# A hybrid decoder step on one core: third head's operands and first loads moved, results of empty slots not stored, two tiles of the per-layer embedding beside the routing, the rest of it in a fixed order

## The chip, the cores and the metric

The kernel runs on one core of a Trainium2 chip. A core has five engines with an instruction queue each: TensorE (PE, matrix products; its weight loads are listed as PEld), VectorE (DVE), ScalarE (ACT), GpSimd (POOL) and SyncE (SP, here an issuer of DMAs). They work from on-chip memory (SBUF), products land in PSUM banks, and 16 DMA engines move data between SBUF and DRAM. The metric is the device time of one execution in microseconds; the time of a kernel is the median of its runs.

## What is computed

One step of a one-layer decoder for 1,024 prompt tokens and 64 sample tokens (8 sequences of 8), width 1,024, all in float32:

```python
h = rmsnorm(x); P = h @ w_in
mix = concat(rwkv7(P), dilated_window_attention(P))     # 8 heads of 64 each
x = x + mix @ w_out
# 1 of 4 groups, then 2 of 8 experts in it: 32 experts of width 256
x = x + sum over the 2 experts of w * (silu(h2 @ w_gate) * (h2 @ w_up)) @ w_down
x = x + (p @ w_ple) * sigmoid(rmsnorm(x) @ w_ple_gate)  # per-layer embedding, p of width 256
y = rmsnorm(x)
```

It also returns the recurrent state and the windows of keys and values. Each token goes to two experts, so 2,176 rows are routed.

## The kernel before

Products are done in three passes: each operand is split into a high part (ACT, L54) and a low part (DVE, L55), and `mm3` (L1348) adds high by high, high by low and low by high. The stages, in order of time:

- Projections (to about 430 us), then the RWKV recurrence in chunks for the prompt. `chain` multiplies the state by its decay on POOL (L779, kept as `self.decay`); a tile of 256 tokens ends with its group norm, whose scale is L871 on POOL.
- Attention of the sample tokens, then of the prompt. The prompt's attention runs in two calls of `phase3`: heads 0 and 1 for the first five blocks, then all heads in pairs, interleaved with the recurrence of the sample tokens (`phase2s`). For each head `head` loads k (L992) and two halves of q (L995) by POOL's queue; a load of 128x1x1024 is 512 KB. Two buffers (`qk3`) serve heads 0, 1, 3, 4, 6, 7, and a pool of its own (`qx3`, on the left side of SBUF) heads 2 and 5. The scores are L1095, bias and maximum L1098, exp L1107, transposes L1118. Before pair `AHEAD` = 2 a hook closes the recurrence's pools and starts the loads of the next stage.
- Output projection and router for nine tiles of tokens. `pre` is a list of weight loads placed one a tile. The last `route` turns logits into experts, weights and ranks (rank products L1499, the weights' exp L1523) and gives `idx`, the token of each expert's slot. Then a branch on the largest count (`overflow`), for experts with more than `CAP` = 96 tokens.
- The experts, a loop written out in order by `phase5`. For each expert POOL gathers 96 rows of the normed tokens (L1611; rows of empty slots are dropped by the bounds check), PE transposes them (L1624), multiplies by gate and up, transposes, and multiplies by `w_down`; ACT copies the result to one of three buffers (`out`, L1661), and POOL stores 96 rows (L1663) to the array `YE` in DRAM. Weights come by SP's queue three experts ahead (L1305, L1306) and, for `w_down`, four (L1330).
- The tail. `embed` multiplies the nine tiles of p by `w_ple` (12 products a tile, copies by ACT L1601 and DVE L1599, stores to `PL`). For each tile POOL gathers its two result rows a token (L1810), DVE adds them (L1819), and norm (L1824, `hp`), transposes (L1834), split (`hh`, `hl`) and the gate product by `w_ple_gate` (`whg`, `whh` and their low parts) follow. The scheduler of the tile framework places these; only `phase5` fixes its order by hand (`self.ordered`, `o`).

The tile framework adds the waits: an instruction waits for the last readers or writers of the memory that it overwrites, and each DMA takes the next of eight semaphores of its kind (DMASW for POOL's, DMAHW for the others).

## Time and profile before

| | |
|---|---|
| runs | 1543.29, 1542.76, 1533.67 us (median 1542.76) |
| the profiled execution | 1534.7 us, span 1533.0 us |
| PE, DVE, ACT, POOL busy | 90%, 62%, 49%, 25% of the span |
| DMA | 344.63 MB, mean 225 GB/s |
| granted clock of PE, mean | 0.951 of full speed |

Times in the views are microseconds from the start of the span. Engines work in their queue's order; in brackets behind a row stands how long the engine was idle before it and what it waited for. Windows give busy time of each engine with the number of its instructions, then PE's granted clock (1.00 is 2.4 GHz, 0.50 is 1.2 GHz), the DMA engines' mean busy share and the rate.

### The profile page before, as it was taken

Reading aid. Unit: us, or ns where it says so; the run is one execution under the profiler, and the core shown is the slowest. Engines: PE = TensorE matmul, PEld = TensorE weight load, DVE = VectorE, ACT = ScalarE, POOL = GpSimd, SP = SyncE. Lnnn points to the kernel's source line nnn. Section 1 sums busy time; section 2 is a strip of 40 time slices with the busy share of each in tenths; the row PEclk is TensorE's granted clock in tenths of the full one; section 3 lists DMA queues with packets and bytes.
Section 4 is the critical chain, followed back from the end, with each engine's and each line's share of the span. In section 5 each row is a group of like instructions: output and inputs, shape, how many; then the busy total and the mean of one; then the engine's idle time right before and its main releaser. Section 6 shows DMA issues by size and latency. Waiting matters only on the chain. (4 is left out here: it accounts for less than half of the span.)

```text
span 1533.0 us, 24768 instructions
## 1 busy us (share of the span) xinstructions
PE 1373.5 (90%) x9127; PEld 1129.0 (74%) x9128; DVE 957.5 (62%) x2146; ACT 749.3 (49%) x1368; POOL 375.6 (25%) x391
## 2 busy tenths in 40 slices
...
DMA  6145566999578465339888755555999999997551
GB/s 212 42 159 170 170 194 196 318 313 311 160 190 221 132 183 162 115 88 158 137 185 248 260 167 177 198 200 197 382 391 384 388 388 390 372 367 241 188 171 69
DMA packets 254271, 344.63 MB, mean 225 GB/s; under 512 B 103918, under 2 KB 183088, under 8 KB 253617
## 3 DMA queue, kind: packets, MB, share of 16 engines
...
q14 instruction: 53, 0.43, 0.1%
...
## 5 line engine op out<-in xcount | busy, mean ns | idle before, releaser
L270 PE MATMUL pj<-hT_hi,wh 128*128 128x384 f32 (+1 forms) x600 | 199.2, 334 | 4.7 <-DVE lora L278 2.7
L270 PE MATMUL pj<-hT_hi,wl 128*128 128x384 f32 (+1 forms) x600 | 199.0, 332 | 0.0
L270 PE MATMUL pj<-hT_lo,wh 128*128 128x384 f32 (+1 forms) x600 | 198.4, 331 | 0.0
L270 PEld LDWEIGHTS pj<-hT_hi,wh 128*128 128x128 f32 x600 | 113.8, 190 | 6.6 <-DVE lora L278 3.0
L270 PEld LDWEIGHTS pj<-hT_hi,wl 128*128 128x128 f32 x600 | 114.0, 190 | 2.4 <-issue 2.2
L270 PEld LDWEIGHTS pj<-hT_lo,wh 128*128 128x128 f32 x600 | 114.2, 190 | 0.6 <-issue 0.2
L690 DVE TENSOR_TENSOR ftmp<-At,X 128x60 f32<-128x60 f32 (+24 forms) x248 | 57.2, 243 | 54.7 <-DMA At<-ABd 18.2
L1611 POOL DMA_INDIRECT x<-HN,idx x32 | 38.3, 1198 | 204.8 <-PE p4t L1624 195.5
L55 DVE TENSOR_TENSOR dl<-draw,dh 128x1024 fp32r<-128x1024 f32 x66 | 80.0, 1216 | 3.6 <-ACT dh L54 3.6
L1095 PE MATMUL pS<-k,q 128*128 128x512 f32 (+2 forms) x192 | 53.7, 393 | 21.7 <-DMA q<-QP 21.1
L54 ACT ACTIVATE dh<-draw 128x1024 fp32r<-128x1024 f32 x66 | 69.0, 1050 | 8.0 <-DMA draw<-in_w_down_dram 8.0
L55 DVE TENSOR_TENSOR wl<-w,wh 128x1024 fp32r<-128x1024 f32 x25 | 35.2, 1408 | 45.0 <-ACT wh L54 44.2
L692 DVE TENSOR_TENSOR X<-X,ftmp 128x60 f32<-128x60 f32 (+24 forms) x248 | 60.4, 256 | 4.2
L779 POOL TENSOR_TENSOR s<-S,pc 128x512 f32<-128x512 f32 x16 | 16.9, 1055 | 180.5 <-DVE S L798 74.3
L1098 DVE CUSTOM_DVE_ANT_0 s<-pS,bias 128x512 f32<-128x512 f32 (+2 forms) x96 | 50.2, 554 | 11.6 <-PE pS L1095 7.9
L1122 ACT ACTIVATE pt<-pxt 128x512 f32<-128x512 f32 (+3 forms) x64 | 32.4, 514 | 50.7 <-PE pxt L1118 50.5
L1118 PE MATMUL pxt<-ident,s 128*128 128x128 f32 x288 | 48.2, 291 | 9.4 <-DVE pt L1120 5.9
L1107 ACT ACTIVATE s<-s,nm 128x128 f32<-128x128 f32 (+7 forms) x64 | 49.2, 770 | 13.3 <-DVE nm L1103 6.8
L1095 PEld LDWEIGHTS pS<-k,q 128*128 128x128 f32 x192 | 32.4, 204 | 30.7 <-issue 22.7
L1348 PE MATMUL p4y<-dh,hh 128*96 128x512 f32 x128 | 54.0, 422 | 0.7 <-ACT hh L54 0.7
L1348 PE MATMUL p4y<-dh,hl 128*96 128x512 f32 x128 | 50.5, 395 | 0.0
L1348 PE MATMUL p4y<-dl,hh 128*96 128x512 f32 x128 | 50.3, 393 | 0.0
...
## 6 DMA issues: line engine op xcount, KB each, us to landing
...
```

The source lines that it names most:

```text
L54: self.hi = self.o(e.activation(hi, src, AF.Copy) if e is nc.scalar else e.tensor_copy(hi, src))
L55: return self.o((lo_eng or nc.vector).tensor_tensor(lo, src, hi.bitcast(F32), op=ALU.subtract))
L270: nc.tensor.matmul(p[:, :nn], a[:, k, :], b[:, k, n0:n0 + nn], start=(m == 0), stop=(m == 23))
L690: nc.vector.tensor_tensor(o, At[:, t, t + 1:32][:, :, None].to_broadcast([128, m, c]), X[:, t, None, 0:c].to_broadcast([128, m, c]), op=AL ...
L692: nc.vector.tensor_tensor(X[:, t + 1:32, 0:c], X[:, t + 1:32, 0:c], o, op=ALU.add)
L1095: nc.tensor.matmul(ps[:, :n], q[:, a, i * 128:(i + 1) * 128], k[:, c0:c0 + n], start=(a == 0), stop=(a == 1))
L1098: nc.vector.tensor_tensor_reduce(s[:, c0:c0 + n], ps[:, :n], bias[:, bo:bo + n], 1.0, -3e38, ALU.add, ALU.max, m)
L1107: ex = nc.scalar.activation(s[:, :nb * 128], s[:, :nb * 128], AF.Exp, bias=nm, accum_out=den)
L1118: nc.tensor.transpose(px[:, b, :], s[:, (b0 + b) * 128:(b0 + b + 1) * 128], self.ident)
L1122: nc.scalar.activation(pt[:, b0:b0 + m, :], px[:, :m, :], AF.Copy)
L1348: self.o(self.nc.tensor.matmul(p, a[x][:, k, :], w, start=(k == 0 and q == 0), stop=(k == kn - 1 and q == 2)))
L1611: d = nc.gpsimd.indirect_dma_start(out=X[e][:n], out_offset=None, in_=self.HN, in_offset=bass.IndirectOffsetOnAxis(ap=self.idx[:, e:e + 1] ...
```

## The change

1. The six arrays of the recurrence in DRAM become views of one tile `R6`, and `YE` becomes its first part.
2. The store of an expert's result becomes a scatter by `row`: row number for a filled slot, a number past the end for an empty one, which the bounds check drops. `row` comes from two more DVE operations behind the routing.
3. `qx3` moves to the right side, and a new pool `qy3` serves head 5, which is loaded only at the hook. The first loads of heads 0 and 1 are ordered ahead of the last decay, and their second parts behind the last tile's scale (L871).
4. `w_ple` is loaded ahead of the routing, and with it tiles 0 and 1 of the embedding are done there; the loads of `w_down` move by one expert, and `w_ple` is loaded again behind the last expert.
5. `embed` does tiles 2 to 8 in a fixed order, with the splits of the first half of `w_ple_gate` between them; its first transposes go into the last step of the experts.

```diff
-        self.XV = t("XV", [4, 128, T])
+        self.R6 = t("R6", [6, 4, 128, T])
+        self.XV = self.R6[0]
         self.ARd = t("ARd", [4, 128, 17, 128])
-        self.KB = t("KB", [4, 128, T])
-        self.BB = t("BB", [4, 128, T])
+        self.KB = self.R6[1]
+        self.BB = self.R6[2]
         self.PC = t("PC", [4, 128, 24])
-        self.BV = t("BV", [4, 128, T])
-        self.AA = t("AA", [4, 128, T])
-        self.GG = t("GG", [4, 128, T])
+        self.BV = self.R6[3]
+        self.AA = self.R6[4]
+        self.GG = self.R6[5]
...
-        nc.gpsimd.tensor_tensor(yv, yv, r[:n, :, None].to_broadcast([n, 8, 64]), op=ALU.mult)
+        m = nc.gpsimd.tensor_tensor(yv, yv, r[:n, :, None].to_broadcast([n, 8, 64]), op=ALU.mult)
+        if t0 == NP - 256:
+            self.scaled = m
...
-            self.qx = ea.enter_context(self.pool("qx3", side="left"))
+            self.qx = e2.enter_context(self.pool("qx3", side="right"))
...
         def after(d):
-            if a:
-                self.tc.add_manual_dep(d.ins, self.decay.ins.name, mybir.DependencyInfo(mybir.DependencyClass.NoSync, mybir.DependencyReason.DATA))
+            x, y = (d, self.scaled) if a else (self.decay, d)
+            if h < 2:
+                self.tc.add_manual_dep(x.ins, y.ins.name, mybir.DependencyInfo(mybir.DependencyClass.NoSync, mybir.DependencyReason.DATA))
         d = nc.gpsimd.dma_start(k[:, a:w], part(self.KP, [[512 * NP, 2], [NP, 64]]))
...
+                    self.qx = P("qy3")
...
-                        self.head(w[0], w[2])
+                        if w[0] != 5 or p == AHEAD:
+                            self.head(w[0], w[2])
...
+    row[:, 149] = j
...
-        self.YE = d.tile([NE * CAP, D], F32, name="YE")
+        self.YE = self.R6.rearrange("s p q t -> (s p q t)")[0:NE * CAP * D].rearrange("(r c) -> r c", c=D)
...
-        r = self.dr[(j // 2 + 1) % 2 if j > 3 else 0].tile([128, 2, D], F32, tag="r", name="draw")
+        r = self.dr[((j + 1) // 2 + 1) % 2 if j > 2 else 0].tile([128, 2, D], F32, tag="r", name="draw")
         if j <= NE:
-            self.hold(self.o(nc.sync.dma_start(r, (I['w_down'][0, j] if j < NE else I['w_ple'][0]).rearrange("(k p) f -> p k f", p=128))), after)
+            self.hold(self.o(nc.sync.dma_start(r, (I['w_down'][0, j] if 0 <= j < NE else I['w_ple'][0]).rearrange("(k p) f -> p k f", p=128))), after)
...
-        pre = [Dn(0), W(0, 0), W(0, 1), Dn(1), W(1, 0), W(1, 1), Dn(2), Dn(3)]
+        pre = [Dn(-1), W(0, 0), W(0, 1), Dn(0), W(1, 0), W(1, 1), Dn(1), Dn(2)]
...
-                    self.split_d((s - 5) // 2, k)
+                    self.split_d((s - 7) // 2, k)
...
+        pe = p4.tile([128, 2, 256], F32, name="pe4")
+        nc.sync.dma_start(pe, I['p_prompt'][0, 0, 0:256].rearrange("(i p) c -> p i c", p=128))
+        self.emb_trans(0, pe, 128, wk.tile([128, 2, 4, 128], F32R, tag="t1", name="ehl"))
         nc.vector.tensor_scalar(self.idx, pidx[:CAP, 0:NE], float(FREE), None, op0=ALU.add)
+        free = p4.tile([CAP, NE], F32, name="free")
+        nc.vector.tensor_scalar(free, pidx[:CAP, 0:NE], 0.0, float(NE * CAP), op0=ALU.is_ge, op1=ALU.mult)
+        nc.vector.scalar_tensor_tensor(self.row, free, row[:CAP], ist[:CAP], op0=ALU.add, op1=ALU.add)
         pr = self.pst("h")
         nc.tensor.matmul(pr[:, :32], ones, macc, start=True, stop=True)
         nc.vector.tensor_copy(self.cnt, pr[:, :32])
+        for i in range(2):
+            self.emb(i, -1, wk.tile([128, D], F32, tag="t3", name="ple"), False)
...
+    def emb_trans(self, j, pe, n, hl):
+        p = self.pst("t").rearrange("p (a b) -> p a b", b=128)
+        m = 4 if j < 4 else 2
+        for q in range(m):
+            self.o(self.nc.tensor.transpose(p[:, q, :n], pe[:n, q // 2, (q % 2) * 128:(q % 2) * 128 + 128], self.ident[:n, :n]))
+        self.split(hl[:, 0, :m, :n], hl[:, 1, :m, :n], p[:, :m, :n])
+        self.E[j] = hl
+    def emb(self, i, w, o, dve=True):
+        nc = self.nc
+        t0, n = TT[i]
+        a = self.E[i // 2][:, :, 2 * (i % 2):2 * (i % 2) + 2, :n]
+        for j in range(2):
+            c = slice(512 * j, 512 * j + 512)
+            p = self.pst("y")
+            self.mm3(p[:n], (a[:, 0], a[:, 1]), self.Dn[w], 0, 2, 2, c)
+            if j and dve:
+                self.o(nc.vector.tensor_copy(o[:n, c], p[:n]))
+            else:
+                self.o(nc.scalar.activation(o[:n, c], p[:n], AF.Copy))
+        self.o(nc.scalar.dma_start(self.PL[t0:t0 + n, :], o[:n]))
+    def embed_first(self):
+        self.emb_trans(1, self.Dn[NE + 1][:, 2:4], 128, self.w2.tile([128, 2, 4, 128], F32R, tag="t5", name="ehl"))
...
     def embed(self):
-        nc, I, wk = self.nc, self.I, self.wk
+        nc, I = self.nc, self.I
         pes = self.Dn[NE + 1]
-        pe8 = self.r4.tile([128, 256], F32, tag="pe", name="pe8", bufs=1)
-        nc.sync.dma_start(pe8[:NS], I['p_sample'][0].rearrange("b t d -> (b t) d"))
+        pe8 = self.r4.tile([128, 1, 256], F32, tag="pe", name="pe8", bufs=1)
+        nc.sync.dma_start(pe8[:NS, 0], I['p_sample'][0].rearrange("b t d -> (b t) d"))
+        self.load_w(NE)
         O = [self.dh.tile([128, 2, D], F32, tag=t, name="ple") for t in "hl"]
...
+        self.ordered = True
+        for i in range(2, 9):
             if i % 2 == 0 and i < 8:
...
+                j = i // 2 + 1
+                self.emb_trans(j, pes[:, 2 * j:2 * j + 2] if j < 4 else pe8, 128 if j < 4 else NS,
+                               self.w2.tile([128, 2, 4, 128], F32R, tag=("t4", "t5")[j % 2], name="ehl"))
+            self.emb(i, NE, O[i // 2 % 2][:, i % 2])
+            if i < 6:
+                self.split_w(NE, i - 2)
+        self.ordered = False
...
-                self.o(nc.gpsimd.dma_start(self.YE[e * n:e * n + n, :], y[:n]))
+                self.o(nc.gpsimd.indirect_dma_start(out=self.YE, out_offset=bass.IndirectOffsetOnAxis(ap=self.row[:, e:e + 1], axis=0),
+                                                    in_=y[:n], in_offset=None, bounds_check=NE * CAP - 1, oob_is_err=False))
...
+        self.load_d(3)
         self.load_d(4)
-        self.load_d(5)
...
-                if e > 1:
+                if e > 0:
                     self.split_d(e, 0)
                 act(e)
...
+            if last:
+                self.embed_first()
+            if e > 0:
                 self.split_d(e, 1) if not last else [self.split_d(e, k) for k in range(2)]
-            if e > 1 and e + 4 <= NE + 1:
+            if e > 0 and e + 4 <= NE + 1:
                 self.load_d(e + 4)
             if ahead:
...
-            self.load_w(NE)
-            for q in range(4):
-                self.split_w(NE, q)
-                self.hold(self.hi, self.last_hh)
             self.load_w(NE + 1)
```

The built order of POOL, between the recurrence of the prompt and that of the samples. k and q are the operands of a head (7962 and 7956 are the third head's), o and LAK belong to the recurrence, ux to the samples'. Before:

```order
L871 TENSOR_TENSOR y<-y,gnr 128x512
L881 TENSOR_TENSOR o_5985<-o_5985,gb 128x512
L659 TENSOR_TENSOR LAK<-LAK,cst 128x512
L992 DMA k_7962<-KP 128x1x1024
L995 DMA q_7963<-QP 128x1x1024 x2
L992 DMA k_8084<-KP 128x1x1024
L995 DMA q_8085<-QP 128x1x1024 x2
L844 TENSOR_TENSOR ux<-vt_99,cst 64x512 x2
L844 TENSOR_TENSOR ux<-us,cst 64x512 x2
L992 DMA k_8208<-KP 128x1x1024
```

And of the change (its lines are two to five further down; 8779 is the sixth head's k):

```order
L873 TENSOR_TENSOR y<-y,gnr 128x512
L997 DMA k_7956<-KP 128x1x1024
L1000 DMA q_7957<-QP 128x1x1024 x2
L885 TENSOR_TENSOR o_5979<-o_5979,gb 128x512
L997 DMA k_8779<-KP 128x1x1024
L661 TENSOR_TENSOR LAK<-LAK,cst 128x512
L1000 DMA q_8780<-QP 128x1x1024 x2
L997 DMA k_8078<-KP 128x1x1024
L1000 DMA q_8079<-QP 128x1x1024 x2
L846 TENSOR_TENSOR ux<-vt_93,cst 64x512 x2
L846 TENSOR_TENSOR ux<-us,cst 64x512 x2
```

The third head's three loads stand ahead of o and LAK instead of behind them, and the sixth head's come next, ahead of the fourth's (8084 before, 8078 now).

POOL at the end of the experts, with waits, from the last but one gather (x) on. Before, y is stored:

```order
L1611 DMA x_14422<-HN,idx 96x1024 [waits DMASW1_49,PE_49]
L1663 DMA YE<-y_14398 96x1024 [waits DMASW0_49,Activation_49]
L1611 DMA x_14526<-HN,idx 96x1024 [waits DMASW3_49,PE_49]
L1663 DMA YE<-y_14502 96x1024 [waits DMASW2_49,Activation_49]
L1663 DMA YE<-y_14606 96x1024 [waits Activation_49]
L1663 DMA YE<-y_14700 96x1024 [waits DMASW4_49,Activation_49]
L1663 DMA YE<-y_14792 96x1024 [waits DMASW5_49,Activation_49]
L1663 DMA YE<-y_14852 96x1024 [waits DMASW6_49,Activation_49]
L1663 DMA YE<-y_14883 96x1024 [waits DMASW7_49,Activation_49]
```

And of the change, where R is the array `R6`:

```order
L1642 DMA x_14530<-HN,idx 96x1024 [waits DMASW7_49,PE_49]
L1694 DMA R_67<-y_14292,row 3072x1024 [waits DMASW4_49,Activation_49]
L1642 DMA x_14636<-HN,idx 96x1024 [waits DMASW1_49,PE_49]
L1694 DMA R_67<-y_14398,row 3072x1024 [waits DMASW6_49,Activation_49]
L1694 DMA R_67<-y_14504,row 3072x1024 [waits DMASW0_49,Activation_49]
L1694 DMA R_67<-y_14610,row 3072x1024 [waits DMASW1_49,Activation_49]
L1694 DMA R_67<-y_14716,row 3072x1024 [waits DMASW3_49,DMASW2_49,Activation_49]
L1694 DMA R_67<-y_14812,row 3072x1024 [waits DMASW3_49,Activation_49]
L1694 DMA R_67<-y_14906,row 3072x1024 [waits DMASW5_49,DMASW4_49,Activation_49]
L1694 DMA R_67<-y_14968,row 3072x1024 [waits DMASW5_49,Activation_49]
L1694 DMA R_67<-y_15009,row 3072x1024 [waits DMASW7_49,DMASW6_49,Activation_49]
```

Behind the last gather stand eight scatters instead of six stores, and each waits for the DMASW semaphore of the scatter ahead of it (DMASW6, 0, 1, 2, 3, 4, 5, 6, each given by the row before), which the stores did not. In the loop a scatter stands behind the gather seven experts on, a store behind that five on.

DVE in the tail, around the first norm product `hp` and the first split `hl` of it. x are the sums of result rows (14895 is the second tile's, xd_15138 the third's), ple copies of the embedding. Before:

```order
L1819 SCALAR_TENSOR_TENSOR x_14895<-y_15133,wgt,x_14895 128x1024
L1824 SCALAR_TENSOR_TENSOR hp_15106<-x_14894,r4r,g_14901 128x1024
L1599 COPY ple<-p4y 128x512 x2
L55 TENSOR_TENSOR ehl<-p4t,ehl 128x2x64
L1819 SCALAR_TENSOR_TENSOR x_14895<-y_15135,wgt,x_14895 128x1024
L1819 SCALAR_TENSOR_TENSOR xd_15138<-y_15183,wgt,xd_15138 128x1024
L1599 COPY ple<-p4y 128x512
L65 TENSOR_SCALAR r4m<-ss_15142 128x1
L1599 COPY ple<-p4y 128x512
L1824 SCALAR_TENSOR_TENSOR hp_15148<-x_14895,r4r,g_14901 128x1024
L55 TENSOR_TENSOR hl_15151<-p4t,hh_15150 128x512 x2
```

And of the change (x_15023 is the second tile's, its second sum; xd_15216 the third's):

```order
L1853 SCALAR_TENSOR_TENSOR x_15023<-y_15213,wgt,x_15023 128x1024
L1858 SCALAR_TENSOR_TENSOR hp_15204<-x_15022,r4r,g_15029 128x1024
L55 TENSOR_TENSOR wlg<-wraw,whg 128x1024
L55 TENSOR_TENSOR ehl<-p4t,ehl 128x2x64
L1608 COPY ple<-p4y 128x512
L1853 SCALAR_TENSOR_TENSOR xd_15216<-y_15261,wgt,xd_15216 128x1024
L55 TENSOR_TENSOR wlh<-wraw,whh 128x1024
L1608 COPY ple<-p4y 128x512
L55 TENSOR_TENSOR wlh<-wraw,whh 128x1024 x3
L65 TENSOR_SCALAR r4m<-ss_15220 128x1
L55 TENSOR_TENSOR hl_15229<-p4t,hh_15228 128x512 x2
```

`hp` stands behind both sums of the second tile instead of one, and five splits of the gate's weights (wlg, wlh), a split of the last tile of p and two copies stand between it and `hl`.

## Rows read from the trace of the kernel before

**Rows 1.** The page: busy time of PE, and the DMA engines' busy tenths in 40 slices of the span.

```profile
PE 1373.5 (90%) x9127; PEld 1129.0 (74%) x9128; DVE 957.5 (62%) x2146; ACT 749.3 (49%) x1368; POOL 375.6 (25%) x391
DMA  6145566999578465339888755555999999997551
```

**Rows 2.** What PE waited for between 690 and 1040 us, the first entry: total, times, longest.

```profile
PE pS L1095 <- DMA q<-QP: 21.1, 4, 10.0
```

**Rows 3.** Timeline of POOL around the loads of the third and the fourth head: start, duration, row, idle time before it.

```profile
689.12 1.13 POOL L779 TENSOR_TENSOR s<-S,pc 128x512 f32<-128x512 f32 x1
...
715.25 1.04 POOL L871 TENSOR_TENSOR y<-y,gnr 128x512 f32<-128x512 f32 x1
...
740.39 0.90 POOL L992 DMA_DIRECT2D k<-KP  x1 [11.86 <-PE po L1052]
...
745.97 0.79 POOL L992 DMA_DIRECT2D k<-KP  x1 [3.10 <-PE pS L1095]
```

**Rows 4.** Timeline of PE: the prompt's last state update, and the end of the second head's scores and the start of the third's.

```profile
706.30 1.06 PE L796 MATMUL s<-u,Bt 128*128 128x128 f32 x8
...
755.97 0.43 PE L836 MATMUL pys<-us,LAB 128*64 128x128 f32 x2
766.23 0.45 PE L1095 MATMUL pS<-k,q 128*128 128x128 f32 x1 [9.83 <-DMA q<-QP]
767.22 0.47 PE L1095 MATMUL pS<-k,q 128*128 128x128 f32 x1 [0.54 <-DMA q<-QP]
```

**Rows 5.** Timelines of ACT and DVE there: the exp of the second head's last block, and the third head's first bias sum.

```profile
755.90 1.04 ACT L1107 ACTIVATE s<-s,nm 128x896 f32<-128x896 f32 x1
...
772.00 0.29 DVE L1098 CUSTOM_DVE_ANT_0 s<-pS,bias 128x128 f32<-128x128 f32 x1 [1.26 <-DMA bias<-in_abase_dram]
```

**Rows 6.** Windows ahead of the wait and in it.

```profile
725.00:740.00 15.00, 14.96 (x152) 13.40 (x152) 8.15 (x31) 8.81 (x22) 1.27 (x1) 1.00 0.16 36
...
750.00:760.00 10.00, 6.40 (x54) 4.90 (x52) 5.17 (x20) 3.87 (x8) 4.16 (x5) 1.00 1.55 216
```

**Rows 7.** The end of the routing: the window, PE's last logits and first rank product, ACT's exp of the weights; and two rows of the embedding in the tail, for the pace of its products at full clock (three from one row's start to the start of the next but one).

```profile
1040.00:1050.00 10.00, 3.31 (x29) 2.88 (x29) 8.00 (x37) 2.94 (x6) 1.65 (x3) 0.67 0.26 106
...
1042.66 1.27 PE L1454 MATMUL p4h<-wrt,ht 128*128 128x36 f32 x8 [1.18 <-DVE r4m L65]
...
1049.08 0.18 PE L1499 MATMUL p4h<-rmm,tri 128*128 128x32 f16 x1 [4.56 <-DVE rmm L1492]
...
1047.90 0.20 ACT L1523 ACTIVATE rdv<-rdv 128x3 f32<-128x3 f32 x1 [2.88 <-DVE rdv L1522]
...
1390.54 0.62 PE L1348 MATMUL p4y<-dh,ehl 128*128 128x512 f32 x2
...
1391.22 0.62 PE L1348 MATMUL p4y<-dh,ehl 128*128 128x512 f32 x2
```

**Rows 8.** Two windows of the expert loop.

```profile
1100.00:1125.00 25.00, 25.00 (x129) 17.75 (x128) 24.45 (x32) 22.23 (x35) 4.01 (x5) 1.00 1.03 395
...
1200.00:1250.00 50.00, 45.63 (x225) 31.62 (x224) 45.68 (x57) 42.29 (x63) 9.71 (x10) 1.00 1.02 389
```

**Rows 9.** Timeline of POOL in the expert loop: the gathers of experts 7, 13 and 31 (the last), the store behind it, and the last store.

```profile
1096.38 0.97 POOL L1611 DMA_INDIRECT x<-HN,idx  x1 [7.21 <-PE p4t L1624]
...
1151.33 0.98 POOL L1611 DMA_INDIRECT x<-HN,idx  x1 [6.58 <-PE p4t L1624]
...
1331.70 0.97 POOL L1611 DMA_INDIRECT x<-HN,idx  x1 [7.21 <-PE p4t L1624]
1333.73 0.55 POOL L1663 DMA_DIRECT2D YE<-y  x1 [1.06 <-ACT y L1661]
...
1378.38 0.51 POOL L1663 DMA_DIRECT2D YE<-y  x1 [6.35 <-ACT y L1661]
```

**Rows 10.** DMA queues from 1100 to 1330 us: packets, MB, share of the 16 engines (q1 holds the weights, q0 gathers and stores).

```profile
q1 hardware_dynamic: 19548, 72.54, 82.0%
q0 software_dynamic: 5345, 16.15, 19.7%
```

**Rows 11.** From issue to landing: of all 32 stores (L1663), of all 32 gathers (L1611), and the median of the four stores between 1340 and 1372 us.

```profile
DMA to landing us min/median/max: 3.5/7.2/8.8
...
DMA to landing us min/median/max: 4.5/7.7/9.6
...
YE<-y POOLq DMA_DIRECT2D x4, 384.0 KB, 6.3
```

**Rows 12.** Timeline of DVE in the tail: four weight splits, the second tile's second sum, the third tile's first sum, a copy, and the first `hl`.

```profile
1374.70 4.62 DVE L55 TENSOR_TENSOR wlg<-wraw,whg 128x1024 fp32r<-128x1024 f32 x4
...
1404.24 1.28 DVE L1819 SCALAR_TENSOR_TENSOR x<-y,wgt,x 128x1024 f32<-128x1024 f32 x1
1408.43 1.28 DVE L1819 SCALAR_TENSOR_TENSOR xd<-y,wgt,xd 128x1024 f32<-128x1024 f32 x1 [2.92 <-DMA y<-YE,slot]
1409.63 0.68 DVE L1599 COPY ple<-p4y 128x512 f32<-128x512 f32 x1
...
1412.76 1.28 DVE L55 TENSOR_TENSOR hl<-p4t,hh 128x512 fp32r<-128x512 f32 x2
```

**Rows 13.** Timelines of ACT and PE in the tail: the last result copies, and the first gate product.

```profile
1377.02 1.06 ACT L1661 ACTIVATE y<-p4y 96x512 f32<-96x512 f32 x2
...
1413.18 0.39 PE L1348 MATMUL p4y<-whg,hh 128*128 128x512 f32 x1
```

30 lines of the change are left out of this document (3 added, 27 removed).

## The prediction

> **What bounds the kernel now.** I read the page first: TensorE (PE) is busy 90% of the span, but the slices of the DMA engines stand at 8 or 9 tenths only in the stretch of the 32 experts [rows 1]. So there are two kernels to think about. Outside the experts PE sets the pace, and a gain is an idle stretch of PE that closes. The list of what PE waited for between 690 and 1040 us shows one entry that matters: 21.1 us for the attention's q operand, in four waits [rows 2]. The timelines show where: PE ends at 756.4 with the second head and starts the third at 766.23, after 9.83 us; POOL could issue that head's k only at 740.39, after 11.86 us of waiting for a PE product of the first attention pass, whose memory the tile took [rows 3, 4]. In the expert loop the DMA is the limit: from 1100 to 1125 PE is busy 25.00 of 25.00 us, from 1200 to 1250 only 45.63 of 50, with the DMA share at 1.02 in both kinds of window and 389 GB/s in the later one [rows 8]. POOL's gathers give the step: 9.16 us while PE sets it (six steps from 1096.38 to 1151.33), and 9.81 on average over the 24 steps to 1331.70 [rows 9]. Behind the experts PE is held by the first tile's chain: result gather, sum, norm, transposes, first gate product at 1413.18 [rows 12, 13]; from there PE works almost without a gap, so what this chain loses, the end loses.
>
> **Third head's operands.** In the built order the third head's k and q stand on POOL right behind the group norm of the last prompt tile, at 715.25 + 1.04 = 716.3, and wait for no PE product any more. The DMA share between 725 and 740 is 0.16 [rows 6], so its three transfers of 128 x 1024 floats, 1.5 MB, land there long before 756. What is late next? Right after the third head's first scores stand transposes of the second head's last block, which need ScalarE's exp, done at 756.94 [rows 5]; that costs 0.5 us of the 10.4 (9.83, and 0.54 in front of the second product [rows 4]). The bias of that head landed so late that VectorE waited 1.26 us for it until 772.00 [rows 5]; it was issued at the same time as now, into a DMA share of 1.55 [rows 6], from which 1.5 MB now go. The fourth head is still issued at 745.97, because it takes the first head's buffer; it is needed 10 us sooner, at about 770, which leaves it 24 us. I take **-10.3**, and as bounds -10.4 and -5 (bias or fourth head late by half of it). The last state decay now stands behind six transfer issues on POOL, at about 704 instead of 689; its reader on VectorE also needs the PE products that start at 706.30 [rows 3, 4], so I cost it at nothing; without that cover it would cost up to 15 us. The second parts of heads 0 and 1 move by one POOL operation (1 us) and their queue slots wait for earlier landings anyway: nothing.
>
> **Two tiles beside the routing.** Their 24 products at 0.227 us (three in 0.68 us [rows 7]) are 5.4 us of PE work for a gap of 4.56 us [rows 7]. The gap itself gets longer: the weight chain's exp, at 1047.90 before, now stands on ScalarE behind three copies of these products, the third of which ends about 18 products (4.1 us) after the last logits at 1043.9 [rows 7], near 1048.8. That is +0.9, and two small VectorE operations for the row numbers and one more split are +0.5: **+1.4**. The window shows a granted clock of 0.67 here [rows 7]; at half clock the 18 products take 8.2 us and the term is +5.5. Lower bound 0.5. Their two stores meet a DMA that is idle.
>
> **Expert loop.** The store of 96 rows becomes a scatter that drops rows of empty slots. That dropped rows are not moved can be read from the gathers: between 1100 and 1330 the software queue moved 16.15 MB [rows 10]; 24 stores of 0.393 MB are 9.44, so 24 gathers moved 0.28 MB each, which is 68 rows (2,176 routed rows / 32), not 96. A scatter saves 28 rows or 0.115 MB per step, 0.29 us at 389 GB/s; PE's own step of 9.16 leaves room for that below 9.81. 27 stores are issued up to 1333.73 [rows 9], before the weights end: -8.0. One more w_down now lies inside the stage (w_ple is loaded ahead in its place, and a second time later): 1.05 MB or +2.7. Together **-5.3**. Bounds: -10 (the software queue's time per MB is larger, 19.7% for 16 MB against 82.0% for 73) and +2.7 (the saving does not reach the weight loads). The one more split on VectorE falls into an early step and is caught up while PE waits for DMA later.
>
> **The scatters' own order.** The built order makes each scatter wait until the one before has landed, and issues it two gathers later than the store. Stores land in 7.2 us (median), gathers in 7.7, at most 9.6 [rows 11]; below the step of 9.5, so the loop is not throttled. But behind the last gather (1331.70) eight scatters are left where six stores were, three of them already overdue, and the last can go only after seven landings. With the stores' 6.3 us at the end of the stage [rows 11], 0.4 for the slower issue (0.97 against 0.55 [rows 9]) and 0.2 for the semaphore, 6.9 each and the first two 7.5, the last scatter goes at about 1380.5 instead of 1378.38, and lands 4 us later: the first result gather starts **+2.5** late. Bounds: 0 (6.2 each, on time) and +6.8 (7.9, as a gather, for the first five).
>
> By the Trainium skill ("DMA: Bandwidth & Descriptors", section "Two DMAs through the same engine are not ordered") only the completion semaphore orders two transfers, which is why overlapping writes have to be serialised like this. It gives no price; the trace of before has no such wait to agree or disagree with.
>
> **Tail.** 24 products fewer (5.4 us) help only where PE is the limit. The order on VectorE now puts the first norm product (hp) behind the second tile's second sum, which ended at 1404.24 + 1.28 = 1405.5, and the first hl behind the third tile's first sum, which ended at 1408.43 + 1.28 = 1409.7, and behind four weight splits of 1.16 and a copy of 0.6 [rows 12]. That gives hl at 1415.0 instead of 1412.76, so +2.3, and with its transposes **+2.5** for the first gate product, at unchanged gathers. PE would be ready sooner (it no longer waits after the last expert), but its three output banks are emptied by the same VectorE queue. Lower bound -1 (the last result copies leave ScalarE sooner, since they stood at 1377.02 behind four splits [rows 13]); upper bound +3.2.
>
> **Sum.** -10.3 + 1.4 - 5.3 + 2.5 + 2.5 = -9.2 us. The profiled execution took 1534.7 us, which gives 1525.5. The three runs shown are 1543.29, 1542.76 and 1533.67, so the profiled one is like the fastest; against their median the sum gives 1533.6, and that is my time.
>
> **Rivals.**
> (a) *The scatters in series throttle the end, slower than before.* For it: eight transfers in a row behind a saturated DMA. Against: landings of 6.3 us there. It decides from 8.2 us a scatter: (1378.4 + 9.2 + 2.5 - 1332.7) / 7, where the last one's delay eats the other gains. At the longest store (8.8, with issue and semaphore 9.4) the last goes at 1398.5, 20 late: -9.2 - 2.5 + 20 = +8, 1551. At the longest gather plus its issue, 10.6, the loop steps at 10.6 too, 24 x 0.8 = +19 more, and the end gets +29: some 1580.
> (b) *The saving does not reach the weights.* The expert term becomes +2.7 and the sum -1.2: 1541.6. For it: the dropped rows are always the last partitions of the tile, so if partitions and DMA engines go together, only some engines get less to do. Against: the mean share of all 16 engines is 1.02 with gathers that drop the same rows [rows 8], so no group of engines is seen idle.
> [...]
> (c) *Everything fits.* Scatters on time, the DMA gain -8 net, the tail +1: -10.3 + 0.5 - 8 + 1 = -16.8, 1526; with the bounds of all terms 1521.
> (d) *The front or the routing gives half back.* The next head or the bias late (-5), or half clock beside the routing (+5.5): sum -4 to -5, 1538.
>
> **Chances.** The forecast (1528 to 1538) 0.40, (c) 0.22, (b) 0.12, (d) 0.11, (a) 0.15. One per cent is 15.4 us, about what a measurement of this kernel can tell from none. Faster by more: most of (c) and, with the spread of 10 us between runs of one kernel, a sixth of the forecast: 0.27. Slower by more: the heavier half of (a), 0.09. Within: 0.64. The range goes from (c)'s bounds, 1521, to the milder (a), 1551; the forecast's own 1528 to 1538 leaves out too much.
>
> **What would show it.** The third head's scores start near 756 with no wait for q; POOL's k at 716. Between the last logits and the first product of the ranks PE shows 24 products, in under 6.5 us. The gathers' mean step falls to about 9.5. The scatters behind the last gather stand 7 us apart, and the last goes some 49 us behind it (46.7 before). On VectorE, hl behind four wlh splits. I am wrong if the steps do not shorten, if a wait for the bias or the fourth head fills the place near 760, or if the last scatter goes over 53 us behind the last gather.

## The result and the profile after

The change takes 1556.61 us (median of 6 runs, 1543.71 to 1566.36) against 1534.99 for the kernel before beside it (6 runs, 1531.06 to 1543.29): ratio 1.0121, 95% interval 1.0083 to 1.0159. By the ratio it is slower by 1.2%, some 18.6 us (21.6 between the medians), where 9.2 us less were forecast; 1556.6 lies above the range of 1521 to 1551. The profiled execution took 1543.71 us (span 1541.6). A second set of runs of the same kernel (e4_changed_again) gave 1558.77 and a profiled span of 1559.9, nearer to the median. So the trace of after is read with that of e4 beside it. A ratio counts only the executions within 1.5% of the fastest of its kernel: five of twelve for the run f2 further down, all or all but one for every other.

A table of six milestones finds the loss. Each column is a stage, in us: **front**, from the span's start to POOL's last store of HN (POOL runs those stores one behind the other, as the routing's tiles get ready); **routing**, from there to the first gather; **loop**, first to last gather; **scatter**, last gather to the first result gather; **gate**, from there to the first gate product on PE that uses `hl` (1413.63 before); **end**, to the end of the span. All are read as starts of rows in the timelines of POOL and PE, and the six add up to the span. The last store of HN and the first gather, before and then after:

```profile
1044.84 0.58 POOL L1459 DMA_DIRECT2D HN<-hn  x1 [1.48 <-ACT hn L1458]
1052.44 1.06 POOL L1611 DMA_INDIRECT x<-HN,idx  x1 [7.02 <-DVE ci L1741]
```

```profile
1035.73 0.58 POOL L1468 DMA_DIRECT2D HN<-hn  x1 [1.48 <-ACT hn L1467]
1045.23 1.08 POOL L1642 DMA_INDIRECT x<-HN,idx  x1 [8.93 <-DVE ci L1774]
```

| kernel | front | routing | loop | scatter | gate | end |
|---|---|---|---|---|---|---|
| before | 1044.8 | 7.6 | 279.3 | 51.0 | 31.0 | 119.4 |
| before again (f1) | 1051.2 | 7.8 | 279.2 | 49.0 | 32.6 | 123.4 |
| after | 1035.7 | 9.5 | 285.8 | 59.2 | 27.6 | 123.8 |
| after again (e4) | 1053.7 | 9.5 | 288.5 | 57.7 | 28.3 | 122.2 |

The loop lost 7 to 9 us and the stretch from the last gather to that gate product (scatter and gate together) some 4.5; the front gained 9 in one execution and gained nothing in the other.

**Front.** The page's busy shares hardly move (PE 90% of the span, as in [rows 1]). The third head's k goes out where it was put, and its scores start without a wait. Timelines of POOL and PE, after:

```profile
716.37 0.90 POOL L997 DMA_DIRECT2D k<-KP  x1
```

```profile
760.84 0.44 PE L1102 MATMUL pS<-k,q 128*128 128x128 f32 x2
```

What PE waits for between 690 and 800 us, the longest entries, first after, then e4 (total, times, longest). Of the four q waits of [rows 2] one long one is left; new is a wait for the values v, short in one execution and 16.4 us in the other:

```profile
PE pS L1102 <- DMA q<-QP: 9.7, 1, 9.7
PE pxt L929 <- DVE an L926: 3.4, 1, 3.4
PE po L1057 <- DMA v<-out_dram: 1.9, 1, 1.9
```

```profile
PE po L1057 <- DMA v<-out_dram: 16.4, 1, 16.4
PE pS L1102 <- DMA q<-QP: 10.6, 2, 10.3
```

SP's queue tells why. It issues the sample state's loads s0s one behind the other, and v stands behind them. Timelines of SP, before, after, e4 (ten or eleven issues take 6.6 us before, and 20 to 22 beside the two heads' loads):

```profile
722.41 6.58 SPq L814 DMA_DIRECT2D s0s<-in_state_wkv_dram  x10
...
739.94 1.01 SPq L1081 DMA_DIRECT2D v<-out_dram  x2
```

```profile
722.86 20.26 SPq L816 DMA_DIRECT2D s0s<-in_state_wkv_dram  x11
...
746.09 1.00 SPq L1088 DMA_DIRECT2D v<-out_dram  x2
```

```profile
723.67 22.04 SPq L816 DMA_DIRECT2D s0s<-in_state_wkv_dram  x11
...
749.40 1.15 SPq L1088 DMA_DIRECT2D v<-out_dram  x2
```

The change sends two heads' operands, not one, into this place: behind the third head's k (716.37) POOL issues the sixth head's (721.50) and its q. The window 725 to 740, with a DMA share of 0.16 in [rows 6], now reads 0.89:

```profile
725.00:740.00 15.00, 13.63 (x142) 12.20 (x142) 7.26 (x29) 8.46 (x20) 2.83 (x3) 1.00 0.89 179
```

In e4 v goes out at 749.40, just behind the fourth head's k at 748.68, and has that head's 1.5 MB ahead of it; in the profiled run of after it slips out at 746.09, ahead of the fourth head (746.55). The other traces agree: where v goes out 0.5 to 0.7 us behind the fourth head's k (e1, e3, h3, e4), PE waits 15.8 to 16.4 us for it, and where it goes out ahead, at most the 1.9 us of after.

**Routing.** VectorE waits 1.79 us for ScalarE's rdv, which stands behind three copies of the new tiles, as forecast. PE's 24 new products take 7.0 us (1034.88 to 1041.9), where under 6.5 were named: the first four start 0.46 us apart and later ones 0.23, and the stage's granted clock is 0.86. Timeline of VectorE, after:

```profile
1041.18 0.16 DVE L1534 SCALAR_TENSOR_TENSOR rgs<-rdv,rgs 128x3 f32<-128x3 f32 x1 [1.79 <-ACT rdv L1532]
```

**Loop.** The queues between 1100 and 1330 us, to be held against [rows 10]: the software queue moves 3.6 MB less (its share falls from 19.7 to 16.3%), and the weights' queue takes that time (82.0 to 83.9%) but moves 1 MB *less*.

```profile
DMA packets 24234, 84.24 MB, mean 366 GB/s; under 512 B 3702, under 2 KB 3702, under 8 KB 24218
## 3 DMA queue, kind: packets, MB, share of 16 engines
q1 hardware_dynamic: 19273, 71.51, 83.9%
q0 software_dynamic: 4945, 12.54, 16.3%
```

**End of the loop.** POOL behind the last gather: eight scatters, which the built order sends one after the landing of the other (for most of them the trace names engines that were long done, for one the DMA itself), the last 54.9 us behind the last gather; [rows 9] had 46.7.

```profile
1331.06 0.99 POOL L1642 DMA_INDIRECT x<-HN,idx  x1 [6.14 <-PE p4t L1655]
1332.36 0.95 POOL L1694 DMA_INDIRECT R<-y,row  x1 [0.31 <-issue]
1341.88 1.07 POOL L1694 DMA_INDIRECT R<-y,row  x1 [8.57 <-ACT whd L54]
1349.44 0.91 POOL L1694 DMA_INDIRECT R<-y,row  x1 [6.49 <-ACT hh L54]
1357.70 1.93 POOL L1694 DMA_INDIRECT R<-y,row  x1 [7.35 <-ACT whf L54]
1366.16 0.91 POOL L1694 DMA_INDIRECT R<-y,row  x1 [6.53 <-DMA R<-y,row]
1373.98 0.91 POOL L1694 DMA_INDIRECT R<-y,row  x1 [6.90 <-ACT hh L54]
1381.64 0.91 POOL L1694 DMA_INDIRECT R<-y,row  x1 [6.75 <-ACT ehl L54]
1385.92 0.91 POOL L1694 DMA_INDIRECT R<-y,row  x1 [3.37 <-ACT ehl L54]
```

ScalarE waits for them too: the first split of the fixed order, ehl, takes the buffer of an earlier expert's result, and waits 7.62 us for its scatter. On VectorE the first hl stands behind four wlh splits, as forecast, and the first gate product that uses it follows at 1417.84. Timelines of ACT, DVE and PE, after (compare [rows 12, 13]):

```profile
1380.98 0.60 ACT L54 ACTIVATE ehl<-p4t 128x512 fp32r<-128x512 f32 x1 [7.62 <-DMA R<-y,row]
```

```profile
1413.63 3.49 DVE L55 TENSOR_TENSOR wlh<-wraw,whh 128x1024 fp32r<-128x1024 f32 x3
...
1417.10 1.28 DVE L55 TENSOR_TENSOR hl<-p4t,hh 128x512 fp32r<-128x512 f32 x2
...
1417.84 0.50 PE L1356 MATMUL p4y<-whg,hl 128*128 128x512 f32 x1 [1.99 <-DVE hl L55]
```

### The profile page after: what moved, and what is told of

It is laid out like the page before. It is cut to its first block, busy times and chain, and to the rows that moved or that the text cites. A ratio compares the mean times of both kernels' runs of the same rounds, so it can differ in the third digit from the quotient of the medians.

```text
span 1541.6 us, 24799 instructions
## 1 busy us (share of the span) xinstructions
PE 1387.2 (90%) x9127; PEld 1136.7 (74%) x9128; DVE 956.3 (62%) x2148; ACT 752.4 (49%) x1372; POOL 402.3 (26%) x391
## 3 DMA queue, kind: packets, MB, share of 16 engines
q0 software_dynamic: 43296, 48.36, 11.1%
## 5 line engine op out<-in xcount | busy, mean ns | idle before, releaser
L1642 POOL DMA_INDIRECT x<-HN,idx x32 | 34.4, 1074 | 209.9 <-PE p4t L1655 197.9
L55 DVE TENSOR_TENSOR dl<-draw,dh 128x1024 fp32r<-128x1024 f32 x68 | 82.4, 1215 | 3.6 <-ACT dh L54 3.5
L54 ACT ACTIVATE dh<-draw 128x1024 fp32r<-128x1024 f32 x68 | 71.1, 1050 | 8.3 <-DMA draw<-in_w_down_dram 8.3
L1102 PE MATMUL pS<-k,q 128*128 128x512 f32 (+2 forms) x192 | 53.1, 390 | 10.4 <-DMA q<-QP 9.7
L1694 POOL DMA_INDIRECT R<-y,row x32 | 45.7, 1427 | 60.5 <-ACT hh L54 13.4
L1356 PE MATMUL p4y<-dl,hh 128*96 128x512 f32 x128 | 50.7, 396 | 0.0
```

What stands on the lines that cost most here:

```text
L54: self.hi = self.o(e.activation(hi, src, AF.Copy) if e is nc.scalar else e.tensor_copy(hi, src))
L55: return self.o((lo_eng or nc.vector).tensor_tensor(lo, src, hi.bitcast(F32), op=ALU.subtract))
L1102: nc.tensor.matmul(ps[:, :n], q[:, a, i * 128:(i + 1) * 128], k[:, c0:c0 + n], start=(a == 0), stop=(a == 1))
L1356: self.o(self.nc.tensor.matmul(p, a[x][:, k, :], w, start=(k == 0 and q == 0), stop=(k == kn - 1 and q == 2)))
L1642: d = nc.gpsimd.indirect_dma_start(out=X[e][:n], out_offset=None, in_=self.HN, in_offset=bass.IndirectOffsetOnAxis(ap=self.idx[:, e:e + 1] ...
L1694: self.o(nc.gpsimd.indirect_dma_start(out=self.YE, out_offset=bass.IndirectOffsetOnAxis(ap=self.row[:, e:e + 1], axis=0), in_=y[:n], in_of ...
```

## The experiments

Ratios are to the kernel before on the same chip, with 95% intervals.

### First set: which part, and is it the scatter?

**e1_plain_store**: the change with the plain store.

```diff
-                self.o(nc.gpsimd.indirect_dma_start(out=self.YE, out_offset=bass.IndirectOffsetOnAxis(ap=self.row[:, e:e + 1], axis=0),
-                                                    in_=y[:n], in_offset=None, bounds_check=NE * CAP - 1, oob_is_err=False))
+                self.o(nc.gpsimd.dma_start(self.YE[e * n:e * n + n, :], y[:n]))
```

> The changed kernel with its scatter put back to a plain store of all 96 rows (into the same part of the shared array; the row numbers are still computed). Theory A (the scatters wait for one another, come late, and hold ScalarE's result copies and the result gathers): the last store again goes about 47 us behind the last gather, and the sum of what is left, front -9, routing +2, one more w_down +3, tail order about +1, gives 1532 us. Theory B (dropped rows relieve only some DMA engines, the weights get slower): the loop returns to about 389 GB/s and the time is also near 1532. Theory C (the loss is the moved w_down load and the tail's order, not the scatter): no better than the changed kernel, 1545 or more.

Measured 1.0073 [1.0041, 1.0106]. **e2_scatter_only**: the kernel before with the same edit the other way, and what it needs (R6, row, free).

> The kernel before with the scatter alone (shared array, row numbers, dropped rows; nothing else of the change). A: the loop loses some 3 us and the end behind the last gather some 8, 1546 us against 1535. B: the same total, with the loss in the loop's rate (about 370 GB/s) and none behind the last gather. C: faster than before by the saved bytes, about 1528.

Measured 1.0079 [1.0055, 1.0103]. **e3_scatter_no_drop**: the change, but every row is stored.

```diff
-        nc.vector.tensor_scalar(free, pidx[:CAP, 0:NE], 0.0, float(NE * CAP), op0=ALU.is_ge, op1=ALU.mult)
+        nc.vector.tensor_scalar(free, pidx[:CAP, 0:NE], 0.0, 0.0, op0=ALU.is_ge, op1=ALU.mult)
```

> The changed kernel with row numbers that never lie past the end, so that the scatter writes all 96 rows, as the store did, and still waits for the scatter before it. A: no faster than the changed kernel, rather a few us slower (longer landings), 1550 to 1565. B: the loop returns to 389 GB/s at even load, some 6 us faster than the changed kernel. C: slower than the changed kernel by the bytes, some 8 us.

Measured 1.0092 [1.0057, 1.0126]. **e4_changed_again**: no edit.

> The changed kernel once more, unchanged, since its six runs lie between 1543.7 and 1566.4 us and the profiled one is the fastest: a second trace shows what differs between its runs. A: the distance from the last gather to the last scatter, and ScalarE's waits for scatters, differ. B: the loop's rate differs. C: neither differs, but another stage.

Measured 1.0105 [1.0064, 1.0146]. None of the three theories holds alone: A and B had e1 near 1532 us (its median is 1555.35), C had e2 near 1528 (1552.79). No single part carries the loss, and storing all rows (e3) or the filled ones (e4) gives the same within the intervals: no gain from the dropped rows is seen.

### Second set: front and embedding apart

**f1_before_again**: no edit. **f2_front_only**: before with the head's part of the change (scaled, qy3, the sixth head's condition). **f3_front_sixth_late**: f2, with the sixth head's load ordered behind a later step of the sample state (ux), which POOL reaches at 784.71 in the kernel before and at 772.81 in f3:

```diff
-                    nc.gpsimd.tensor_tensor(ux[q], src[q, None, q].to_broadcast([64, 8, 64]),
+                    self.uxs.append(nc.gpsimd.tensor_tensor(ux[q], src[q, None, q].to_broadcast([64, 8, 64]),
...
-            if h < 2:
+            if h == 5:
+                x, y = d, self.uxs[4]
+            if h < 2 or h == 5:
```

**f4_embed_only**: before with the two tiles beside the routing, the loads moved, the fixed order of the rest, and R6, row and free, but plain stores.

> The kernel before, unchanged: a second trace of it, since its profiled run is among its fastest. Ratio 1.00. Theory B says its loop again shows 16.15 MB on the software queue and about 386 GB/s between 1100 and 1330; if it shows 376 or less, the loop's rate varies by itself and the loops of the other traces have to be compared with this one.

> The kernel before with the moved operands and loads alone (third head's pool, sixth head's pool, first loads). Theory D, from four traces of kernels that hold this part: the third and the sixth head's 3 MB fill the DMA between 717 and 746, the sample states' loads on SyncE's queue are dragged out (20 us in place of 7), and the v load behind them is issued some 7 us later and lands behind the fourth head's 1.5 MB; PE waits 16 us for v in most runs and 2 in few. By D the ratio is about 1.003 (+5 us; -8 in the lucky runs). By the prediction's term it is 10 us faster (0.993).

> The same with one more order on GpSimd's queue: the sixth head's loads stand behind the second sample block's first product of masks (near 785, where the kernel before had them). By D the states' loads take about 7 to 12 us again, v is issued near 740 and PE waits for neither v nor q: 8 to 10 us faster than before (0.994). If the third head's load alone is enough to delay v, the ratio stays at 1.00 or above.

> The kernel before with the embedding's part alone (two tiles beside the routing, w_ple loaded twice, fixed order in the tail; plain stores, the old front). Terms of the prediction for it: routing +1.4, one more w_down +2.7, tail order +2.5: 1.004. From the trace of the changed kernel: routing +1.9, and 4 us of waits behind the first gate product: 1.005. If it is 1.00 or below, the tail's order pays for its terms.

Measured: f1 0.9984 [0.9962, 1.0005]; f2 0.9953 [0.9912, 0.9995]; f3 0.9898 [0.9871, 0.9926]; f4 1.0103 [1.0074, 1.0132], above the 1.004 to 1.005 expected. The twelve executions of f2 lie between 1520.09 and 1549.15 us, with a median of 1543.86, which is 1.0029 of the kernel before beside it (1539.45), as theory D has it. The traced one took 1547.03 and has a wait of 17.8 us for v, issued 3.1 us behind the fourth head's k. With the sixth head out of the way SP's loads end sooner, v goes out at 740.31 and the wait for v is gone from PE's list. Timeline of SP, f3:

```profile
723.00 15.02 SPq L814 DMA_DIRECT2D s0s<-in_state_wkv_dram  x11
...
740.31 1.00 SPq L1089 DMA_DIRECT2D v<-out_dram  x2
```

f3 (1525.19, at most 1527.0) is the fastest kernel of the study, faster than the kernels before and after. And f4, with neither scatter nor front, costs as much as everything together: loop 288.7 us. Parts that each cost some 9 us in the loop alone (e2 287.8, f4 288.7, f1 279.2) and no more together should share something.

### Third set: the place of the result rows in DRAM

**g1_rows_in_six**: before with the rows over R6, nothing else. **g2_embed_own_rows**: f4 with the rows in a tile of their own. **g3_scatter_own_rows**: e2 with a tile of their own, all rows stored. The edit of g1 (g2 and g3 have it the other way):

```diff
+        self.R6 = t("R6", [6, 4, 128, T])
-        self.XV = t("XV", [4, 128, T])
+        self.XV = self.R6[0]
...
-        self.YE = d.tile([NE * CAP, D], F32, name="YE")
+        self.YE = self.R6.rearrange("s p q t -> (s p q t)")[0:NE * CAP * D].rearrange("(r c) -> r c", c=D)
```

> The kernel before with one edit: XV, KB, BB, BV, AA and GG are cut from one DRAM tile R6, and the experts' result rows (YE) lie in R6 over them, stored by the same plain copies; no scatter, no other part of the change. The embedding part alone and the scatter alone each lengthened the expert loop (288.7 and 287.8 us from first to last gather, 279.2 in the kernel before), and together no more (285.8 to 288.5); what both had in common is this place of the rows. Theory E (the place of the rows slows every transfer of the loop a little): first to last gather 286 to 289 us, weights' queue under 0.38 MB per busy microsecond of the 16 engines against 0.386, ratio 1.005 to 1.010. Theory F (the loop is longer by the parts' own work, one w_down fewer held ahead and the scatters): 279 to 280 us, ratio 0.997 to 1.003.

> The embedding part alone as in the run before (1.0103), but the result rows in a DRAM tile of their own as in the kernel before, plain stores. Theory E: first to last gather back to 279 to 282 us and ratio 0.998 to 1.004, since what is left is routing +1.8, the last gather to the first result gather, and the tail order -2 to -3. Theory F: 288 to 289 us and 1.009 to 1.011, as before; the seventh step of the loop 15 us again.

> The kernel before with its plain stores turned into row scatters of all 96 rows of each expert (none dropped) into a DRAM tile of their own; no other part of the change. Theory E: the loop gets 279 to 283 us, and the scatters in series behind the last gather cost what they cost before (last gather to last scatter 53 to 55 us, 46.7 with plain stores), ratio 1.003 to 1.006. Theory F (scatters slow the weights by themselves): 286 to 289 us, ratio 1.007 to 1.011.

Measured: g1 1.0014 [0.9994, 1.0033], loop 277.9; g2 1.0104 [1.0082, 1.0127], loop 287.2; g3 1.0100 [1.0073, 1.0127], loop 287.4. Theory E falls: the place in DRAM costs nothing that the interval shows. But the slow ones still share an edit: the tile row.

### Fourth set: the tile row and what lies behind it

The compiled programs give SBUF addresses, as the expectations of h1 and h2 quote them: row takes 128 bytes a partition, and every tile behind it starts 128 bytes lower, wraw at 210816 in place of 210944 (a multiple of 512). **h1_shift_128** is before with only that; **h2_shift_256** has `2 * NE` in it; **h3_change_padded** is the change with a wider row; **h4_change_padded_late** is h3 with f3's edit.

```diff
+        self.nc.gpsimd.memset(c4.tile([CAP, NE], I32, name="row"), 0)
```

```diff
-        self.row = c4.tile([CAP, NE], I32, name="row")
+        self.row = c4.tile([CAP, 4 * NE], I32, name="row")[:, 0:NE]
```

> The kernel before with one more small tile beside idx (96 x 32 int32, 128 bytes a partition, set to zero once and never read), nothing else. The change's new tile row has this size and place, and every tile allocated behind it in SBUF (the weights' landing buffers wraw and draw, the gathered rows, the experts' results) then starts 128 bytes lower: wraw at 210816 in place of 210944, so on no multiple of 256 bytes any more. Theory G (the start addresses slow every transfer of the loop): first to last gather 286 to 289 us against 279, 374 to 379 GB/s in the loop against 387 to 390 at the same busy share, ratio 1.004 to 1.008. Theory H (the tile is innocent; the scatters and the embedding part each cost the loop by themselves): 278 to 280 us, 387 to 390 GB/s, ratio 0.998 to 1.002.

> As the run h1_shift_128, with the unread tile twice as large (256 bytes a partition), so that the landing buffers start on multiples of 256 bytes that are no multiples of 512 (wraw at 210688). The Trainium skill, page DMA: Bandwidth & Descriptors, section How a descriptor splits into AXI transactions, states that a descriptor that does not start on a multiple of 256 bytes has one more transaction and fetches bytes that it does not use. Theory G with 256 bytes as the boundary: 278 to 280 us from first to last gather and ratio 0.998 to 1.002. Theory G with 512 bytes as the boundary: 286 to 289 us and 1.004 to 1.008. Theory H: 278 to 280 us as well.

> The whole change with one edit: the tile row is allocated four times as wide (512 bytes a partition, of which the first 32 columns are used), so that every tile behind it starts on a multiple of 512 bytes again, as in the kernel before. Theory G: first to last gather 277 to 281 us and ratio 1.004 to 1.008, some 6 to 9 us less than the change as it is (1.0105 to 1.0121); what is left is the v load of the front (+14 in most executions against the gain of 9), the routing (+1.9), the scatters in series (+8). Theory H: 285 to 289 us and 1.009 to 1.013, as without the padding.

> The whole change, padded as in h3_change_padded, and with the sixth head's load ordered behind the third of the sample state's steps as in f3_front_sixth_late (that edit alone took the front's part from 0.9953 to 0.9898). Theory G: 0.996 to 1.001, PE without a wait of over 10 us for v near 767 us and the loop at 277 to 281 us. Theory H: 1.001 to 1.006. In either case slower than f3_front_sixth_late (0.9898), since the routing and the scatters in series still cost their 2 and 8 us.

Measured: h1 1.0062 [1.0036, 1.0088]; h2 1.0005 [0.9981, 1.0029]; h3 1.0096 [1.0061, 1.0131]; h4 1.0009 [0.9988, 1.0031]. An unread tile of 128 bytes costs 0.6%, one of 256 bytes nothing that the interval shows. First and last gather on POOL, h1 and then h2 (286.3 us against 279.7), and their queues from 1100 to 1330 us, with f1's last:

```profile
1055.69 1.06 POOL L1612 DMA_INDIRECT x<-HN,idx  x1 [7.16 <-DVE ci L1742]
...
1341.97 1.44 POOL L1612 DMA_INDIRECT x<-HN,idx  x1 [7.21 <-PE p4t L1625]
```

```profile
1050.26 1.07 POOL L1612 DMA_INDIRECT x<-HN,idx  x1 [7.52 <-DVE ci L1742]
...
1329.94 1.16 POOL L1612 DMA_INDIRECT x<-HN,idx  x1 [7.20 <-PE p4t L1625]
```

```profile
DMA packets 24245, 86.53 MB, mean 376 GB/s; under 512 B 3154, under 2 KB 3154, under 8 KB 24229
## 3 DMA queue, kind: packets, MB, share of 16 engines
q1 hardware_dynamic: 19079, 70.78, 81.7%
```

```profile
DMA packets 24825, 88.66 MB, mean 385 GB/s; under 512 B 3214, under 2 KB 3214, under 8 KB 24809
## 3 DMA queue, kind: packets, MB, share of 16 engines
q1 hardware_dynamic: 19596, 72.72, 82.2%
```

```profile
DMA packets 25117, 89.65 MB, mean 390 GB/s; under 512 B 3268, under 2 KB 3268, under 8 KB 25099
## 3 DMA queue, kind: packets, MB, share of 16 engines
q1 hardware_dynamic: 19877, 73.74, 82.7%
```

The mark is in MB per share, not in the share: the weights' queue moves 0.866 MB per per cent shifted by 128 bytes (70.78 / 81.7), 0.885 by 256, and unshifted 0.885 (before) to 0.892 (f1). All kernels with plain stores fall into the same two groups: 0.866 to 0.872 shifted (h1, e1, f4, g2), 0.884 to 0.892 not (before, f1, f3, g1, h2, i1, i3). The share is the time that packets took and can pass one ([rows 6] has 1.55), so this says that each transfer took longer. The engines' own work on the landed data did not: the splits of w_down between 1100 and 1330 us take 1215 ns on VectorE in h1 and h2, and 1048 and 1049 ns on ScalarE. Which of the shifted buffers matters was not taken apart.

The Trainium skill ("DMA: Bandwidth & Descriptors", section "How a descriptor splits into AXI transactions") states that a transaction starts on a multiple of 256 bytes, and that a descriptor that does not start there begins with one from the multiple below, of which the bytes ahead of its start are fetched, unused, and still cost beats. An estimate from that page for a row of 4 KB shifted by 128 bytes is 17 transactions for 16 and 132 beats for 128, or 3.1%. The page speaks of what is fetched; here the shifted side is the one written, for which it states nothing. The runs agree in kind: 256 is harmless (0.885 for 0.884 to 0.892), and 128 costs 1.4 to 2.9%, less than the estimate.

h3's loop is back to 280.2, but its ratio, above the 1.004 to 1.008 expected, does not show it: in its trace the front has the wait for v (15.8 us) and the routing took 11.1 us. h4, without the v wait, is 0.87% below h3 and in its range.

### Fifth set: what is left of each part

**i1_embed_padded**, **i2_scatter_padded**: f4 and e2 with the wide row. **i3_change_mended_plain**: h4 with e1's plain store.

> The embedding part alone as in f4_embed_only (1.0103: plain stores, the old front), with the tile row padded to 512 bytes a partition. Theory G (the 1 percent of that run was mostly the shifted landing buffers): first to last gather back from 288.7 to 278 to 281 us, ratio 1.000 to 1.004; what is left is routing +1.8 and the end between -3 and +2. Theory H (what the embedding part does in the loop costs by itself): over 284 us and 1.006 to 1.010.

> The scatter alone as in e2_scatter_only (1.0079: empty slots' rows not stored, the old front, the old embedding), with the tile row padded to 512 bytes a partition. Theory G: the loop from 287.8 to 278 to 281 us; the scatters still land some 7 us apart behind the last gather, so last gather to first result gather stays at 56 to 59 us against 51 of the kernel before; ratio 1.002 to 1.005, of which all is the scatters in series. If the rows that are not stored helped the weights, the loop would be under 276 us.

> The whole change with three edits: the sixth head's load late (as f3_front_sixth_late), row padded to 512 bytes a partition, and the results stored by the plain copies of the kernel before (all rows stored). By the account so far: the front's -10 as in f3_front_sixth_late (0.9898), routing +1.9, loop as before, no scatters in series, the end -2 to -3: ratio 0.987 to 0.992, 7 to 9 us under h4_change_padded_late (1.0009), which still has the scatters. If it stays above 0.996, the embedding part costs something that the account does not have.

Measured: i1 1.0046 [1.0022, 1.0069], loop 278.9; i2 1.0067 [1.0037, 1.0096], loop 282.3; i3 0.9961 [0.9940, 0.9983], loop 280.6. All three lie above their ranges. i1 is 0.57% under f4, so a good half of f4's 1% was the shift. i2's loop is 5.5 us shorter than e2's, its ratio little lower. i3 is 0.6% above f3; its trace has 3.4 us more in the routing (11.1 for 7.7), 1.5 in the loop and 2.9 behind the last gather, but a front 6.7 us shorter, so one trace of each does not settle where the 0.6% are. By its expectation a ratio above 0.996 says that the embedding part costs something that the account does not have. The longer end in the next table is such a cost.

The traces of all five sets, read as the six stages above, give one table for the terms. f2's trace, of an execution longer than its median, stands outside (loop 279.5, scatter and gate 84.8, front 1049.9, end 123.0).

| stage | kernels | us |
|---|---|---|
| loop, not shifted | before, f1, f3, g1, h2, h3, h4, i1, i2, i3 | 277.9 to 282.3 |
| loop, shifted by 128 bytes | after, e1 to e4, f4, g2, g3, h1 | 285.8 to 289.1 |
| scatter + gate: old order, plain store | before, f1, f3, g1, h1, h2 | 81.2 to 84.4, mean 82.6 |
| the same, new order, plain store | e1, f4, g2, i1, i3 | 81.7 to 83.6, mean 82.5 |
| the same, old order, scatter | e2, g3, i2 | 87.4 to 89.8, mean 88.2 |
| the same, new order, scatter (the change) | after, e3, e4, h3, h4 | 85.6 to 87.1, mean 86.5 |
| front: old | before, f1, e2, f4, g1 to g3, h1, h2, i1, i2 | 1040.5 to 1051.2, mean 1045.9 |
| front: the change's | e1, e3, e4, h3; after | 1050.0 to 1053.7; 1035.7 |
| front: sixth head late | f3, h4, i3 | 1026.2 to 1032.8 |
| routing: old | all without the embedding's tiles | 7.6 to 8.2 |
| the same, with the tiles, at a granted clock of 0.99; 0.86; 0.78 | g2; after, e1, e3, e4, f4, h4, i1; h3, i3 | 7.9; 9.5; 11.1 |
| end: old order | the nine kernels of it above | 119.4 to 123.9, mean 122.0 |
| end: new order | the ten kernels of it above | 122.2 to 126.5, mean 124.6 |

## Why the prediction was wrong

**Front, -10.3.** The mechanism was right: no wait for q at the third head, and in the execution with a short wait for v a front 10.2 us below the old fronts' mean (1035.7 against 1045.9). That the two numbers agree so well is partly luck: the old fronts alone spread over 11 us, the wait of 9.83 was 15.2 in f1 and 14.8 in g1, and by its own terms (10.4 less 0.5) the sum is -9.9. The step that failed is "What is late next?". It named the bias and the fourth head. It looked at POOL's queue and the DMA share, and not at SP's, where v stands behind ten state loads; nor did it count the sixth head's 1.5 MB, which the change moves as well. In four of five traces PE waits 15.8 to 16.4 us for v and the front ends at 1050 to 1054, 4 to 8 us *later* than the old mean. f3 shows it by moving only the sixth head's loads (median 1525.19 against f2's 1543.86), and h4 shows it again (1539.50 against h3's 1558.48).

**Routing, +1.4.** Measured +1.6 (9.5 against a mean of 7.9), by the wait that was named. The half clock of rival (d) came in part: the stage takes 7.9 us at a granted clock of 0.99, 9.5 at 0.86 and 11.1 at 0.78.

**Expert loop, -5.3.** Two failures. The -8.0 for dropped rows did not come; in this the outcome is that of rival (b). With all rows (e3) or the filled ones (e4) the loop is 286.7 and 288.5, and unshifted with dropped rows 280.2 to 282.3, where plain stores give 277.9 to 280.6. The bytes did fall (12.70 MB in the software queue of i2 against 15.69 in f1), but the weights' queue took the freed time: it moved 0.857 MB per per cent of its share against 0.884 to 0.892. This loss goes with the dropped rows and not with the scatter as such. Scatters of all rows (e3, g3) have 0.860 to 0.866 in the shifted place, close to the plain stores there (0.866 to 0.872), and scatters that drop rows 0.841 to 0.852 (e2, e4, after). In the same way packets under 512 bytes rise from 3268 (f1) to 3709 (i2) only where rows are dropped; e3 has 3123. Queues from 1100 to 1330 us, i2 and then e3:

```profile
DMA packets 24426, 85.00 MB, mean 370 GB/s; under 512 B 3709, under 2 KB 3709, under 8 KB 24410
...
q1 hardware_dynamic: 19437, 72.11, 84.1%
q0 software_dynamic: 4973, 12.70, 16.0%
```

```profile
DMA packets 24219, 86.57 MB, mean 376 GB/s; under 512 B 3123, under 2 KB 3123, under 8 KB 24202
...
q1 hardware_dynamic: 19383, 71.90, 83.0%
q0 software_dynamic: 4819, 14.45, 18.1%
```

Why is open: filled rows in plain stores were not tried, so neither these packets nor the uneven load of rival (b) is shown. The prediction's argument against (b) does not hold either, since a mean share of 1.02 leaves no engine idle only if the share cannot pass one, and [rows 6] has 1.55. The second failure weighs about as much: +7 to +8, for which there was no term at all. The prediction costed row by its two VectorE operations, and not by the 128 bytes that it takes ahead of all landing buffers. h1 has that alone: 286.3 us, +0.62%. The +2.7 for one more w_down shows at most in part (i1 278.9, i3 280.6).

**Scatters in series, +2.5, and tail, +2.5.** Together +5.0; measured +3.9 up to the product with `hl` (86.5 against 82.6), and 2.6 more in the end, which was held to lose only what the chain ahead of it loses. At the end the granted clock is 0.92 to 0.95 with the new order and 0.94 to 0.97 with the old; whether that is all of it is open. The division was wrong: the first result gather starts 7.4 us later behind the last gather (means 58.1 and 50.7), over the bound of 6.8, and the way from there to `hl` is 3.4 us shorter. By the table, the scatters alone cost 5.6 up to `hl`, the new order alone nothing. The mis-sized price is that of one scatter: 6.9 us each were forecast (of which 0.2 for the semaphore stands in no row), and the steps of after are 7.6 to 9.5 us, the last 4.3. The sum itself is short as well: seven landings at its prices are 49.5 us, which from a first scatter at 1332.7 gives 1382.2 and not 1380.5. So in after, e3 and e4 the last one stands 53 to 55 us behind the last gather, over the 53 named as the mark of error, and ScalarE's ehl waits 7.62 us for a buffer that such a scatter still reads.

**Sum.** By the means: front +5.6 (where v is late), routing +1.6, loop +8 (287.2 in after and e4, 279.2 unshifted with plain stores), last gather to `hl` +3.9, end +2.6, together some +22; measured 18.6 by the ratio and 21.6 between the medians. For the profiled execution of after, with its front of -10, the same terms give +6; it took 1543.7, and the medians of before lie between 1535.0 and 1541.9 in the six sets of runs.
